# Down projection of an encoder layer: one token tile's share of product 7 moved between two tiles of product 4

## The chip, the cores and the metric

The kernel runs on one core of a Trainium2 chip. The core has five engines with queues of their own: TensorE (PE in the profile; its weight loads are shown as PEld), VectorE (DVE), ScalarE (ACT), GpSimd (POOL) and SyncE (SP), which issues most of the DMAs. Each engine takes its instructions in the order in which they were written, and engines wait for each other through semaphores. TensorE writes its results to PSUM, eight banks of 128 partitions by 512 float32 values here, and VectorE or ScalarE read them from there.

The metric is the device time of one execution in microseconds. The comparison is between the median of several runs of the kernel before and of the changed kernel. The profile is one execution, recorded by the hardware profiler.

## What is computed

The reference is one layer of a bidirectional encoder over 1024 tokens of width 1024: a mixing part (retention and windowed attention), a first layer norm that gives `h`, then a gated feed-forward part with a small embedding term, and a second layer norm.

```python
g = jnp.einsum('bsd,df->bsf', h, w_ffn_gate[i])
up = jnp.einsum('bsd,df->bsf', h, w_ffn_up[i])
ffn = jnp.einsum('bsf,fd->bsd', jax.nn.silu(g) * up, w_ffn_down[i])
...
h = _layer_norm(ALPHA * h + ffn + ple_gate * ple, ln2_gain[i], ln2_bias[i])
```

The change lies in the last two lines: the down projection (the product of the 1024 x 2816 hidden values with `w_ffn_down`, 2816 x 1024) and the second layer norm of the finished rows.

## The kernel before

**Matmuls in parts.** Each float32 operand is split into a high part and a rest (`split`, L74: ScalarE writes the high part on L75, VectorE the rest on L76), and a product takes three matmuls: high by high, high by rest, rest by high (`mm3c`, L891 to L893). Each has 128 x 128 stationary and 128 x 512 moving values.

**Seven products.** The down projection is computed with seven products in place of eight (a Strassen-like scheme on 2 x 2 blocks: two halves of the tokens, two halves of the hidden values, two halves of the output columns). A product `p` takes a combination of blocks of the hidden values (loaded from the scratch tensor `ad`) and a combination of blocks of `w_dn` (loaded, and summed by DMAs on GpSimd's queue that add in memory, L1222). `AIN` (L1188) says which part each product takes.

**Units.** The hidden dimension is cut in 11 pairs of 128-row blocks, in two segments: `SEG` (L1187) has pairs 0 to 4 and 5 to 10. A unit is one product for one pair; `seq` (L1401) gives the order, in which the second segment ends with products 3, 7 and 4. There are 77 units (`ND`). A unit has four steps: `dload` issues its loads, `dprep` splits its two operands into two slots of the ring `"op"`, `mm` does its matmuls for four token tiles of 128 rows, and `post` runs at the last pair of a product.

**Slots.** The ring `"op"` has 22 slots of one split operand each, taken in turn, so that a slot comes back after eleven units. `dprep` runs up to ten units ahead of `mm` (L1459 to L1461).

**Banks.** The four token tiles of a product accumulate in four PSUM banks. Products 6, 7 and 4 of the second segment share their four banks (`GRP`, L1360): product 7 adds to what product 6 left there, product 4 to both. At the end of products 6 and 7 `dpost` (L1362) adds or subtracts the banks as they then stand into the accumulators `accd` in SBUF (`addto`, L1274).

**The lower tiles and the upper tiles.** `accd` 0 to 3 are token tiles of the first half, 4 to 7 of the second. Tiles 4 to 7 are finished after product 3; their layer norm is laid out in `later` (L1390 to L1394), of which one list is popped in each of the following steps: `squares` and a multiply on ScalarE, `rstd` with a power on GpSimd (L1312), a product with the gain on VectorE (L1337), and an addition of the bias by DMA (L1338).

**The end.** The last product, 4, isn't done pair by pair over the four tiles: `products(t)` does its six pairs for one tile, and `tail` (L1342) goes through tiles 0 to 3, so that the layer norm of a tile runs beside the matmuls of the next. Its parts, on VectorE unless noted: `addto` with sums, `var` (mean, and for tiles 0 to 2 the squares on ScalarE, L1295), `rstd` (two small instructions, then the power on GpSimd), `center` (subtract the mean, times the gain, L1317, two halves), `scale` (times the reciprocal deviation, plus bias, L1322, two halves, each followed by its store on SP's queue, L1323). Tile 3 (`LAST`) takes its sums with `bn_stats` (L1282, L1301).

**Order.** From the gate and up projection on, PE, DVE, Activation, Pool and SP are under `manual_schedule` (L1468): each engine's queue has the order in which the program writes its instructions.

**Buffers `R`.** `dpost` of product 1 keeps four tiles of the tag `"w"` (L1369), from which twelve DMAs on GpSimd's queue add into the accumulators (L1376).

Of the kernel before, what the change touches and what calls it, by code (L numbers as in the profile page):

```python
# [10 lines left out]
F32R = mybir.dt.float32r  # L11
# [5 lines left out]
P = 128  # L17
# [4 lines left out]
HF = 512  # L22
# [20 lines left out]
def layer(tc, xT, xn, w_first, w_mt, w_rv, w_out, w_pg, w_pe, pT, w_gu, w_dn,  # L43
# [11 lines left out]
    wp = cstack.enter_context(tc.tile_pool(name="wp", bufs=4))  # L55
# [3 lines left out]
    def nm(s):  # L59
        uid[0] += 1  # L60
        return f"{s}{uid[0]}"

    def bank(tag, shape=(P, HF)):
        return ps.tile(list(shape), F32, tag=tag, bufs=NB[tag], name=nm("b" + tag))
# [36 lines left out]
    def rawt(w):  # L101
        return wp.tile([P, w], F32, tag="raw", bufs=2, name=nm("raw"))
# [51 lines left out]
    with tc.manual_schedule(engines={mybir.EngineType.DVE, mybir.EngineType.SP}):  # L154
        for kt in range(KT):
            r = xraw[kt]
# [25 lines left out]
            w = wf[kt % 2]  # L182
# [316 lines left out]
    class Attention:  # L499
# [62 lines left out]
        def half(self, hh):  # L562
            return self.y[:, hh * HF:(hh + 1) * HF].rearrange("p (n c) -> p n c", n=4)
# [76 lines left out]
    def ytile(k):  # L640
        ys[k] = a_tile([P, S], "y", "A0" if k < 4 else "A1")
        return ys[k]
# [39 lines left out]
    with tc.manual_schedule(engines={mybir.EngineType.PE}):  # L682
# [11 lines left out]
        r = Retention(0, y0)  # L694
# [6 lines left out]
        for i in range(1, NPAIR):  # L701
# [3 lines left out]
            r = Retention(i, ytile(2 * i))  # L705
# [19 lines left out]
    for n, k in enumerate(order):  # L725
        if n % 2 == 0:
            yp = big16()
        t = yp[:, :, n % 2, :]
# [64 lines left out]
    for kt in range(4):  # L793
        if kt % 2 == 0:
            wbig = ct([P, 2, 2, 2, HF], ("h2", "h3")[kt // 2], dt=F32R)
        r = rawt(2 * HF)
# [92 lines left out]
    def mm3c(o, lh, ll, rh, rl, start, stop):  # L889

        pe.matmul(o, lh, rh, start=start, stop=False, skip_group_check=True)  # L891
        pe.matmul(o, lh, rl, start=False, stop=False, skip_group_check=True)  # L892
        pe.matmul(o, ll, rh, start=False, stop=stop, skip_group_check=True)  # L893
# [269 lines left out]
    n = 0  # L1163
# [23 lines left out]
    SEG = [list(range(0, 5)), list(range(5, NP))]  # L1187
    AIN = {1: (3, 1), 2: (1, 1), 3: (1, 0), 4: (0, 1), 5: (2, 0), 6: (0, 0), 7: (3, 0)}  # L1188
    rings = {"op": [], "a": [], "chain": [], "b": []}
    turn = {k: 0 for k in rings}  # L1190
# [62 lines left out]
    def dmm(p, n, k, ts, first, stop):  # L1253

        a, b = dops[p, n]
        for t in ts:
            c = slice(t * P, (t + 1) * P)
            mm3c(dbank[k][t], a[:, 0, c], a[:, 1, c], b[:, 0, :], b[:, 1, :], first, stop)
# [8 lines left out]
    def pop():  # L1267
        for f in later.pop(0):
            f()
# [4 lines left out]
    def addto(t, h, b, op=ALU.add, done=False):  # L1274


        if done and t != LAST and op == ALU.add:
            dve.tensor_tensor_reduce(half(t, h), half(t, h), b, 1.0, 0.0, op, ALU.add, stts[t][:, h:h + 1])
            return
        dve.tensor_tensor(half(t, h), half(t, h), b, op)  # L1280
        if done and t == LAST:
            dve.bn_stats(stts[t][:, 6 * h:6 * h + 6], half(t, h))  # L1282
        elif done:
            act.activation(ct([P, HF], "sg", 2), half(t, h), AF.Copy, accum_out=stts[t][:, h:h + 1])

    LAST = 3

    def negmean(t):
        stt = stts[t]
        dve.tensor_scalar(stt[:, 12:13], stt[:, 0:1], stt[:, 1:2], -1.0 / D, ALU.add, ALU.mult)  # L1290

    def squares(t):
        stt = stts[t]
        for h in range(2):
            act.activation(ct([P, HF], "sg", 2), half(t, h), AF.Square, bias=stt[:, 12:13], accum_out=stt[:, 2 + h:3 + h])  # L1295

    def var(t):

        stt = stts[t]
        if t == LAST:  # L1300
            dve.bn_aggr(stt[:, 12:14], stt[:, 0:12])  # L1301
            dve.tensor_scalar(stt[:, 12:13], stt[:, 12:13], -1.0, None, ALU.mult)
        else:
            negmean(t)
            squares(t)

    def rstd(t):
        stt = stts[t]
        if t != LAST:
            dve.tensor_scalar(stt[:, 13:14], stt[:, 2:3], stt[:, 3:4], 1.0 / D, ALU.add, ALU.mult)  # L1310
        dve.tensor_scalar(stt[:, 14:15], stt[:, 13:14], EPS, None, ALU.add)
        pool.tensor_tensor(stt[:, 15:16], stt[:, 14:15], cst[:, C_MH:C_MH + 1], ALU.pow)  # L1312

    def center(t):
        for h in range(2):
            x = half(t, h)
            dve.scalar_tensor_tensor(x, x, stts[t][:, 12:13], ln2[0][:, hs[h]], ALU.add, ALU.mult)  # L1317

    def scale(t):
        for h in range(2):  # L1320
            x = half(t, h)
            dve.scalar_tensor_tensor(x, x, stts[t][:, 15:16], ln2[1][:, hs[h]], ALU.mult, ALU.add)  # L1322
            sp.dma_start(out[t][:, hs[h]], x)  # L1323
# [18 lines left out]
    def tail(products):  # L1342

        bs = dbank[len(SEG) - 1, GRP[4]]
        for t in range(4):
            products(t)
            if t:
                rstd(t - 1)
            addto(t, 0, bs[t], done=True)
            var(t)  # L1350
            if t < LAST:
                if t:
                    scale(t - 1)
                center(t)
        rstd(LAST)
        scale(LAST - 1)
        center(LAST)
        scale(LAST)

    GRP = {1: 0, 2: 0, 5: 1, 3: 1, 6: 2, 7: 2, 4: 2}  # L1360
# [1 line left out]
    def dpost(p, s, t):  # L1362

        last = s == len(SEG) - 1
        b = dbank[s, GRP[p]][t]
        if p == 1:
            if s == 0:
                if t % 2 == 0:
                    R.append([wp.tile([P, 2, HF], F32, tag="w", bufs=4, name=nm("R")) for _ in range(2)])  # L1369
                act.activation(R[t // 2][0][:, t % 2], b, AF.Copy)  # L1370
            else:
                r, n = (x[:, t % 2] for x in R[t // 2])
                dve.tensor_tensor(r, r, b, ALU.add)
                act.activation(n, r, AF.Copy, scale=-1.0)
                for tt, h, x in ((t, 0, r), (t + 4, 1, n), (t, 1, n)):
                    later.append([lambda o=half(tt, h), x=x: pool.dma_start(o, x, accum_op=ALU.add)])  # L1376
        elif p == 2:
            addto(t + 4, 0, b, done=last)
        elif p == 5:
            addto(t, 1, b)  # L1380
        elif p == 6:
            addto(t + 4, 1, b, ALU.subtract)
        elif p == 3:
            addto(t + 4, 1, b, done=last)
            if last:
                negmean(t + 4)
                if t == 0:
                    squares(4)
            if last and t == 3:
                f, m, w = ([x[i] for x in map(ln2_steps, range(4, NT))] for i in range(3))  # L1390
                q = [None] + [lambda u=u: squares(u) for u in range(5, NT)]
                later.extend([[], [q[1], f[0]], [m[0], w[0], q[2], f[1]], [m[1], w[1], q[3], f[2]], [m[2], f[3]], [m[3]],
                              [w[2], w[3]]])
                later[-1].extend(lambda u=u: sp.dma_start(out[u], accd[u]) for u in range(4, NT))  # L1394
        elif p == 7:
            addto(t, 1, b, ALU.subtract, done=last)
        else:
            addto(t, 0, b)


    seq = [(1, 0), (5, 0), (2, 0), (3, 0), (6, 0), (1, 1), (7, 0), (2, 1), (4, 0), (5, 1), (6, 1), (3, 1), (7, 1), (4, 1)]  # L1401
# [4 lines left out]
    def d_units(p, s):  # L1406
        k, first, grp, last = (s, GRP[p]), p in (1, 5, 6), SEG[s], (p, s) == seq[-1]

        def mm(n):
            if first and n == grp[0]:  # L1410
                tg = dsets[which[k]]
                dbank[k] = [bank(tg[t // 2]) for t in range(4)]
            if not last:
                dmm(p, n, k, range(4), first and n == grp[0], n == grp[-1])
            elif n == grp[-1]:
                def products(t):
                    for q in grp:
                        dmm(p, q, k, [t], False, q == n)

                while later:  # L1420
                    pop()
                tail(products)

        def post(n):
            if n == grp[-1] and not last:
                for t in range(4):
                    dpost(p, s, t)

        for n in grp:
            dunits.append((lambda n=n: dload(p, n), lambda n=n: dprep(p, n), lambda n=n: mm(n), lambda n=n: post(n)))  # L1430
# [4 lines left out]
    NG, ND = len(gunits), len(dunits)  # L1435
# [10 lines left out]
    def load_ln2():  # L1446
        for j in range(2):
            g = ct([P, D], "u", 4)
            sp.dma_start(g, lnp[2 + j].partition_broadcast(P))
            ln2.append(g)  # L1450

    def d_step(k):
        dunits[k][2]()
        dunits[k][3]()
        if later and k < ND - 6:
            pop()
        while stores and stores[0][0] <= NG + k:
            stores.pop(0)[1]()
        pa = min(10, 5 + k // 3)  # L1459
        ahead(0, k + 1 + pa + 4)  # L1460
        ahead(1, k + 1 + pa)  # L1461
        if k in (2, 3, 4, 5, 8, 9, 10, 11):
            load_acc()
        if k == ND - 24:
            load_ln2()

    ET = mybir.EngineType
    with tc.manual_schedule(engines={ET.PE, ET.DVE, ET.Activation, ET.Pool, ET.SP}):  # L1468
# [112 lines left out]
```

## Time and profile before

| what | value |
|---|---|
| runs | 1204.84 us median of 3 (1204.73 to 1205.9) |
| profiled execution | 1208.0 us, its span 1206.2 us |
| mean granted TensorE clock | 0.998 |
| DVE busy | 735.6 us (61%) |
| ACT busy | 507.6 us (42%) |
| POOL busy | 363.1 us (30%) |
| HBM read and written | 124.67 MB and 47.45 MB |

The span goes from the first to the last instruction of the profiled execution; the rest of its time lies around it. In a row of the timeline stand the start, the duration, the engine, the line, the operation, the tiles written and read, how many instructions are merged, and in brackets how long the engine was idle before and what released it. In a row of the stretches stand the length, the busy time and number of instructions of each engine, the granted clock, the busy share of the DMA engines and GB/s. The end of a matmul is modelled; the spacing of starts is what TensorE delivers.

### The profile page before, as it was taken

The numbers are of one execution on the slowest core, as the hardware profiler recorded it, in microseconds if no ns is written. First come the engines' busy times: TensorE is split into PE (matmuls) and PEld (weight loads), VectorE is DVE, ScalarE is ACT, GpSimd is POOL, SyncE is SP. The second block draws the span as 40 slices with busy tenths as digits, with TensorE's granted clock in tenths as the row PEclk, the third lists the DMA queues.
The fourth block names the chain that finished last, engine by engine and source line by source line (L and its number), as shares of the span: only waits on it lengthen the run. The fifth ranks groups of instructions, "written<-read, shape, count | busy, mean of one in ns | idle before, by whom it ended". The sixth has DMA issues, their size and how long they took to land.

```text
span 1206.2 us, 16452 instructions
## 1 busy us (share of the span) xinstructions
PE 1192.5 (99%) x5940; PEld 994.1 (82%) x5940; DVE 735.6 (61%) x1262; ACT 507.6 (42%) x958; POOL 363.1 (30%) x342
## 2 busy tenths in 40 slices
PE   9999999999999999999999999999999999999997
PEld 6888888888888888888888888888888888888885
DVE  4633788866645387946855554455554565775677
ACT  4665237665775124303423323233323324562463
POOL 2001020202010021001765565646656432034232
PEclk9999999999999999999999999999999999999999
DMA  6233635410103216656233222332133159999976
GB/s 249 83 110 141 249 135 195 151 40 20 35 18 122 91 50 229 255 202 220 89 132 131 79 79 105 131 132 79 63 121 131 70 178 300 375 274 218 258 178 199
DMA packets 70034, 178.45 MB, mean 148 GB/s; under 512 B 8128, under 2 KB 12352, under 8 KB 69952
## 3 DMA queue, kind: packets, MB, share of 16 engines
q1 hardware_dynamic: 61312, 160.61, 37.3%
q0 software_dynamic: 8640, 16.78, 8.0%
q8 instruction: 47, 0.77, 0.3%
q14 instruction: 35, 0.29, 0.1%
HBM read 124.67 MB, written 47.45 MB: 143 GB/s over the span
## 4 chain that ended last, share of the span: by engine, by line
PE 95%; DVE 2%; DMA 1%; issue 1%; ACT 1%; DVEq 0%; SPq 0%; ACTq 0%
PE bmm L81 7%; PE bmm L83 7%; PE bmm L82 7%; PE bs L893 5%; PE bs L891 5%; PE bs L892 5%; PE bmm L891 5%; PE bmm L892 5%; PE bmm L893 5%; PE bt L891 5%; PE bt L893 5%; PE bt L892 5%; PE bo L891 4%; PE bo L893 4%; PE bo L892 4%; PE bo L557 2%
## 5 line engine op out<-in xcount | busy, mean ns | idle before, releaser
L81 PE MATMUL bmm<-H,w 128*128 128x512 f32 x240 | 97.0, 404 | 1.4 <-ACT H L75 1.4
L83 PE MATMUL bmm<-H,w 128*128 128x512 f32 x240 | 94.4, 393 | 0.0
L82 PE MATMUL bmm<-H,w 128*128 128x512 f32 x240 | 94.0, 392 | 0.0
L1050 POOL TENSOR_TENSOR H<-ln 128x512 f32<-128x512 f32 x22 | 28.9, 1313 | 180.9 <-ACT w L75 98.0
L76 DVE TENSOR_TENSOR w<-raw,w 128x512 fp32r<-128x512 f32 x64 | 51.0, 804 | 51.3 <-ACT w L75 50.8
L1080 POOL TENSOR_TENSOR ev<-ev 128x512 f32<-128x512 f32 x33 | 55.0, 1666 | 90.5 <-DVE ev L1095 39.4
L76 DVE TENSOR_TENSOR w<-H,w 128x512 fp32r<-128x512 f32 x44 | 41.0, 932 | 62.5 <-ACT w L75 62.5
L518 POOL COPY sc<-skb 128x1 f32<-128x1 f32 x64 | 14.3, 229 | 193.0 <-PE bt L545 143.9
L1078 ACT ACTIVATE ev<-ev 128x512 f32<-128x512 f32 x33 | 20.9, 632 | 102.7 <-DVE ev L1095 102.7
L1084 POOL TENSOR_TENSOR ev<-ev,ev 128x512 f32<-128x512 f32 x44 | 62.7, 1437 | 2.6
L76 DVE TENSOR_TENSOR u<-H,u 128x512 fp32r<-128x512 f32 x47 | 36.7, 781 | 37.7 <-ACT u L75 37.4
L81 PEld LDWEIGHTS bmm<-H,w 128*128 128x128 f32 x240 | 45.2, 188 | 11.6 <-ACT H L75 2.4
L83 PEld LDWEIGHTS bmm<-H,w 128*128 128x128 f32 x240 | 45.2, 188 | 10.0
L523 DVE CUSTOM_DVE_ANT_0 sc<-cst,bs,skb 128x384 f32<-128x384 f32 (+1 forms) x64 | 34.8, 577 | 28.8 <-PE bs L522 27.0
L75 ACT ACTIVATE w<-raw 128x512 fp32r<-128x512 f32 x64 | 39.3, 624 | 30.2 <-PE bo L83 12.4
L82 PEld LDWEIGHTS bmm<-H,w 128*128 128x128 f32 x240 | 45.3, 189 | 7.8
L527 ACT ACTIVATE sc<-sc,st 128x385 f32<-128x385 f32 (+1 forms) x64 | 37.2, 584 | 32.2 <-DVE st L525 32.2
L75 ACT ACTIVATE u<-H 128x512 fp32r<-128x512 f32 x47 | 29.6, 630 | 44.6 <-PE bs L893 8.1
L763 POOL TENSOR_TENSOR stt<-stt,cst 128x1 f32<-128x1 f32 x8 | 11.6, 1456 | 101.0 <-DVE stt L762 101.0
L479 POOL TENSOR_TENSOR sm<-sm,cst 128x8 f32<-128x8 f32 x8 | 14.3, 1783 | 88.3 <-DVE sm L478 88.3
L1054 POOL TENSOR_TENSOR H<-raw,H 128x512 f32<-128x512 f32 x22 | 37.3, 1697 | 0.0
L1051 POOL TENSOR_TENSOR H<-H,raw 128x512 f32<-128x512 f32 x22 | 35.7, 1624 | 1.7
(807 smaller groups left out, 3748.1 us busy)
## 6 DMA issues: line engine op xcount, KB each, us to landing
ad<-ev SPq DMA_DIRECT2D x33, 512.0 KB, 2.6
pgd<-pro SPq DMA_DIRECT2D x28, 512.0 KB, 2.9
raw<-in_w_gu SPq DMA_DIRECT2D x22, 512.0 KB, 4.3
ln<-in_w_gu SPq DMA_DIRECT2D x22, 512.0 KB, 3.6
raw<-ad SPq DMA_DIRECT2D x40, 256.0 KB, 5.8
ln<-ad SPq DMA_DIRECT2D x37, 256.0 KB, 6.2
H<-in_w_dn SPq DMA_DIRECT2D x33, 256.0 KB, 6.1
raw<-in_w_mt SPq DMA_DIRECT2D x14, 512.0 KB, 3.8
```

The lines of the kernel that those rows point to most:

```text
L75: act.activation(hi, raw, AF.Copy)
L76: dve.tensor_tensor(lo, raw, hi.bitcast(F32), ALU.subtract)
L81: pe.matmul(o, lh, rh, start=start, stop=False)
L82: pe.matmul(o, lh, rl, start=False, stop=False)
L83: recent[0] = pe.matmul(o, ll, rh, start=False, stop=stop).ins.name
L527: act.activation(sc[g][:, :nk + 1], sc[g][:, :nk + 1], AF.Exp, bias=st_[:, 1, j, g:g + 1], accum_out=st_[:, 2, j, g:g + 1])
L891: pe.matmul(o, lh, rh, start=start, stop=False, skip_group_check=True)
L892: pe.matmul(o, lh, rl, start=False, stop=False, skip_group_check=True)
L893: pe.matmul(o, ll, rh, start=False, stop=stop, skip_group_check=True)
L1054: pool.tensor_tensor(s[3], a(0, 1), s[0], ALU.subtract)
L1080: pool.tensor_tensor(c[:, 1, :], c[:, 0, :], c[:, 1, :], ALU.mult)
L1084: pool.tensor_tensor(self.ev[dst][:, 0, :], left, right, op)
```

## The change

Product 7 of the second segment, the last but one, does its six pairs for tiles 0 to 2 alone, and `dpost` reads those three banks. Its part for tile 3 is now a call of `products(7, t)` in `tail`, between tiles 2 and 3 of product 4, followed by `scale(2)` and by the `dpost` of that tile. `rstd(2)` is written ahead of the moved matmuls; `scale(2)` is written between them and the matmuls of product 4 for tile 3; `rstd(3)` now comes behind `center(3)`. At step `ND - 32` four tiles of the tag `"w"` are put into the ring `"op"`, at the place that is next in turn, so that the ring has 26 slots.

```diff
         bs = dbank[len(SEG) - 1, GRP[4]]
         for t in range(4):
-            products(t)
-            if t:
+            if t == LAST:
+                rstd(t - 1)
+                products(7, t)
+                scale(t - 1)
+                dpost(7, len(SEG) - 1, t)
+            products(4, t)
+            if 0 < t < LAST:
                 rstd(t - 1)
             addto(t, 0, bs[t], done=True)
             var(t)
-            if t < LAST:
-                if t:
-                    scale(t - 1)
-                center(t)
+            if 0 < t < LAST:
+                scale(t - 1)
+            center(t)
         rstd(LAST)
-        scale(LAST - 1)
-        center(LAST)
         scale(LAST)
...
+        tiles = range(3 if (p, s) == seq[-2] else 4)
+
         def mm(n):
...
             if not last:
-                dmm(p, n, k, range(4), first and n == grp[0], n == grp[-1])
+                dmm(p, n, k, tiles, first and n == grp[0], n == grp[-1])
             elif n == grp[-1]:
-                def products(t):
+                def products(p, t):
                     for q in grp:
                         dmm(p, q, k, [t], False, q == n)
...
             if n == grp[-1] and not last:
-                for t in range(4):
+                for t in tiles:
                     dpost(p, s, t)
...
+        if k == ND - 32:
+            r, pos = rings["op"], turn["op"] % len(rings["op"])
+            r[pos:pos] = [wp.tile([P, 2, HF], F32R, tag="w", bufs=4, name=nm("w")) for _ in range(4)]
+            turn["op"] = pos
```

## The prediction

> **What bounds the kernel now.** I read the page's busy shares first, then the table of stretches over the last 42 us, then the end of the chain of work that ended last.
>
> ```profile
> PE 1192.5 (99%) x5940; PEld 994.1 (82%) x5940; DVE 735.6 (61%) x1262; ACT 507.6 (42%) x958; POOL 363.1 (30%) x342
> ...
> 1164.50:1180.80 16.30, 16.30 (x73) 13.51 (x72) 11.89 (x31) 12.10 (x25) 5.64 (x10) 1.00 0.48 103
> 1180.80:1197.30 16.50, 16.50 (x73) 13.33 (x71) 14.18 (x30) 8.06 (x20) 2.93 (x6) 1.00 0.84 236
> 1197.30:1206.20 8.90, 0.00 (x1) 0.00 (x0) 5.78 (x11) 0.00 (x0) 1.48 (x2) 0.73 0.36 133
> ```
>
> The columns of the last three rows are PE, PEld, DVE, ACT and POOL. TensorE is full until 1197.3: product 7 fills 1164.50 to 1180.82, product 4 the rest. Then 8.9 us follow without it, in which VectorE finishes token tile 3 and the last store lands. So the time is matmul time, plus any hole in it, plus that tail. The end of the chain:
>
> ```profile
> 1197.34 0.70 DVE acc L1280
> 1198.06 0.71 DVE stt L1282
> ...
> 1199.25 1.32 DVE acc L1322 x2
> 1200.57 0.72 DVE acc L1317 x2
> ...
> 1201.81 0.74 DVE acc L1322
> ```
>
> The 1.32 us of L1322 at 1199.25 are `scale(2)`, work of another tile inside tile 3's tail. The change takes it out of there, and pays with TensorE's order.
>
> **The matmuls.** They are neither added nor removed. The TensorE timeline gives their spacing:
>
> ```profile
> 1164.50 0.39 PE L891 MATMUL bs<-u,u 128*128 128x512 f32 x1
> ...
> 1180.82 0.39 PE L891 MATMUL bs<-H 128*128 128x512 f32 x1
> ...
> 1193.06 0.39 PE L891 MATMUL bt<-H 128*128 128x512 f32 x1
> ...
> 1196.92 0.39 PE L893 MATMUL bt<-u,u 128*128 128x512 f32 x1
> ```
>
> 72 matmuls take 16.32 us, 0.2267 each; one token tile of one product (six operands, three matmuls each) takes 18 of them, 4.08 us. Product 7 on three tiles thus ends its issue at 1164.50 + 54 x 0.2267 = 1176.74, 4.08 earlier than now, and 4.08 us of product 7 come back after product 4's third tile. Without a hole TensorE would end where it does now.
>
> **First hole, before product 4.** Products 6, 7 and 4 accumulate in the same four banks, and `dpost` has to read a bank between 7 and 4. What VectorE does there now:
>
> ```profile
> 1176.64 1.23 DVE L1337 TENSOR_TENSOR acc<-acc,u 128x1024 f32<-128x1024 f32 x1 [1.98 <-ACT acc L1334]
> 1177.78 0.21 DVE L1310 TENSOR_SCALAR stt<-stt 128x1 f32<-128x1 f32 x1
> ...
> 1178.33 0.15 DVE L1311 TENSOR_SCALAR stt<-stt 128x1 f32<-128x1 f32 x1
> 1178.98 1.37 DVE L1280 TENSOR_TENSOR acc<-acc,bs 128x512 f32<-128x512 f32 x2 [0.50 <-PE bs L893]
> ```
>
> At 1178.98 it reads tile 0's bank, after 0.50 us of waiting for TensorE. That 0.50 is all the slack. Ahead of the read in the same queue stand the upper tiles' normalizing steps, and these go by their own chain, not by TensorE:
>
> ```profile
> 1175.13 0.20 POOL L1331 TENSOR_TENSOR stt<-stt 128x1 f32<-128x1 f32 x1
> 1175.36 1.25 ACT L1334 ACTIVATE acc<-acc,stt 128x1024 f32<-128x1024 f32 x1 [1.51 <-POOL stt L1331]
> ```
>
> GpSimd's L1331 ends at 1175.33 and releases ScalarE's L1334 0.03 later, which releases VectorE's L1337 at 1176.64. Further back this chain hangs on a DMA: the last split ahead of product 3's evictions waited for its operand.
>
> ```profile
> 1162.59 0.63 ACT L75 ACTIVATE H<-h0b 128x512 fp32r<-128x512 f32 x1 [0.59 <-DMA h0b<-in_w_dn]
> ```
>
> So taking product 7's fourth tile away moves TensorE up and not VectorE. The read can begin 0.07 after the start of the L1311 at 1178.33 (0.06 is what an independent instruction follows it by in the rows of the tail, below), at 1178.40, and ends 0.69 later (half of the 1.37 for two), at 1179.09. What a matmul pays when VectorE releases it shows in one place:
>
> ```profile
> 578.19 1.77 DVE L76 TENSOR_TENSOR w<-H,w 128x512 fp32r<-128x512 f32 x1
> ...
> 580.02 0.50 PE L893 MATMUL bs<-H,w 128*128 128x512 f32 x1 [0.35 <-DVE w L76]
> 580.36 0.39 PE L891 MATMUL bs<-H,w 128*128 128x512 f32 x1
> ```
>
> It starts 0.06 after VectorE's end (579.96), and the next one follows after 0.34 instead of 0.23: 0.11 more. Product 4 therefore starts at 1179.15 instead of 1176.74, and the hole is 2.41 + 0.11 = **2.52 us**. The evictions of tiles 1 and 2 end at 1180.5, long before their banks are written. Tile 0 of product 4 then ends about 1183.5; VectorE is free for it when the last L1337 is through:
>
> ```profile
> 1180.08 2.38 ACT L1334 ACTIVATE acc<-acc,stt 128x1024 f32<-128x1024 f32 x2 [2.06 <-POOL stt L1331]
> ...
> 1189.18 0.69 DVE L1278 CUSTOM_DVE_ANT_0 acc<-acc,bs 128x512 f32<-128x512 f32 x1 [0.34 <-PE bs L893]
> ```
>
> 1182.46 + 1.23 = 1183.7. These 0.2 us are taken up by the 0.34 for which VectorE waits ahead of the next tile, and cost nothing.
>
> **Second hole, before tile 3 of product 4.** The moved 18 matmuls end 4.08 us after product 4's tile 2. Their bank must again be read by VectorE before product 4 may add to it, and here nothing else is left for TensorE. What is queued in front of that read, by the rows of tile 2 now:
>
> ```profile
> 1193.26 0.69 DVE L1278 CUSTOM_DVE_ANT_0 acc<-acc,bt 128x512 f32<-128x512 f32 x1 [0.17 <-PE bt L893]
> ...
> 1194.12 1.40 DVE L1322 SCALAR_TENSOR_TENSOR acc<-acc,stt,u 128x512 f32<-128x512 f32 x2
> ...
> 1195.45 1.41 DVE L1317 SCALAR_TENSOR_TENSOR acc<-acc,stt,u 128x512 f32<-128x512 f32 x2
> ...
> 1196.77 0.21 DVE L1310 TENSOR_SCALAR stt<-stt 128x1 f32<-128x1 f32 x1
> 1197.01 0.15 DVE L1311 TENSOR_SCALAR stt<-stt 128x1 f32<-128x1 f32 x1
> 1197.25 0.55 POOL L1312 TENSOR_TENSOR stt<-stt,cst 128x1 f32<-128x1 f32 x1 [3.53 <-DVE stt L1311]
> ```
>
> `addto(2)` starts 0.20 after the slot in which TensorE's next matmul goes out (1193.06). From there to the end of GpSimd's L1312 is 4.54 (1197.80), all of it one chain: sums, mean, `scale(1)`, `center(2)`, `rstd(2)`. Then come, in the new order, `scale(2)`, which is 0.03 behind GpSimd (as L1334 behind L1331) and lets the next instruction start after 1.33 (1194.12 to 1195.45), and only then the read of tile 3's bank, 0.69. Sum from the free slot: 0.20 + 4.54 + 0.03 + 1.33 + 0.69 = 6.79, and 0.06 to release TensorE: 6.85. The moved matmuls cover 4.08 of it. The hole is 2.77, with the slow second matmul 0.11 more: **2.88 us**. Of the 6.79, what has no row is the empty VectorE behind L1312; its length is that of GpSimd's power, for which there are eight cases:
>
> ```profile
> L1312 POOL TENSOR_TENSOR stt<-stt,cst x8: 545/560/1341, 1169.0 to 1199.3; 128x1 f32<-128x1 f32 x8
> ```
>
> I take the 0.55 of tile 2's row above; with 1.34 the hole is 0.8 larger. From below: had VectorE nothing in front of the read, the hole would be 0.20 + 0.69 + 0.06 + 0.11 = 1.06. The bn_stats that follows the read lies beside the last 18 matmuls, as do the two stores of `scale(2)` on SP's queue.
>
> **The tail.** After its mean (L1302) tile 3 now goes on with `scale(2)`, and the power runs beside that:
>
> ```profile
> 1199.04 0.15 DVE L1302 TENSOR_SCALAR stt<-stt 128x1 f32<-128x1 f32 x1
> 1199.11 0.14 DVE L1311 TENSOR_SCALAR stt<-stt 128x1 f32<-128x1 f32 x1
> 1199.17 1.40 DVE L1322 SCALAR_TENSOR_TENSOR acc<-acc,stt,u 128x512 f32<-128x512 f32 x2
> ```
>
> Afterwards `center(3)` follows L1302, and `rstd(3)` has been moved behind it, so that the power is no longer covered by anything. From `addto(3)` to the first half of `scale(3)` it is now 1201.81 - 1197.34 = 4.47. Then: L1302 ends at 1.85, `center(3)` starts at 1.88, L1311 follows it by 1.32 at 3.20 and ends at 3.35, GpSimd starts 0.09 later (1197.16 to 1197.25) and ends at 3.99, `scale(3)` starts at 4.02. **Gain 0.45 us** of the 1.32 that left; the rest goes to the uncovered power. With the slowest power (1.34) it is a loss of 0.34. From `scale(3)` on nothing changes.
>
> **The four slots.** They are the buffers of `R`, whose last additions are DMAs on GpSimd's queue. Twelve operands of product 7 stay alive to the end now, so without the slots the last split would overwrite one. The buffer that comes free last goes to the split that stands here at 1129.44 and waits for its own DMA:
>
> ```profile
> 1117.20 0.87 POOL L1376 DMA_DIRECT2D acc<-R  x1 [2.72 <-issue]
> ...
> 1129.44 0.64 ACT L75 ACTIVATE H<-h 128x512 fp32r<-128x512 f32 x1 [2.17 <-DMA h<-in_w_dn]
> ...
> DMA to landing us min/median/max: 4.4/5.6/8.9
> ```
>
> The last of the twelve additions is issued at 1117.20; the slowest landing gives 1126.1, the median 1122.8. I cost the wait at nothing; its cover is 3.3 to 6.6 us. If that is gone, what queues behind is every later split on ScalarE and VectorE, and through them the chain of the first hole.
>
> **Sum.** 2.52 + 2.88 - 0.45 = +4.95 us on the profiled span of 1206.2, so 1211.1. That execution took 1208.0 with what lies around the span, 3.2 over the runs' median of 1204.84; I put the difference on the median: 1204.84 + 4.95 = **1209.8 us**, 0.4% slower.
>
> **Rivals.**
>
> *Only the second hole.* The first one depends on when the upper tiles' chain lets VectorE go, and that hangs on DMA landings (1162.59). If the chain runs 2.5 us earlier in the changed kernel, which has more slots and so splits sooner, 2.88 - 0.45 = +2.4 remain: 1207.3. Against it: ScalarE's waits there are for DMAs, not for slots.
>
> *Not slower.* One mechanism: VectorE is early enough that the read of a bank follows its last matmul at once. Its place is the read of tile 3; from 1.8 us less in front of it on, nothing but the 1.06 is left, and with the first hole gone too the sum is 1.06 - 0.45 = +0.6: 1205.4. For it speaks only that VectorE is 14.18 of 16.50 us busy in that stretch, not full; against it that the 4.54 are a chain of dependences. That the change does what it says without any wait of TensorE would give -0.45, 1204.4; the shared bank excludes it.
>
> *The clock falls in the holes.* The profile shows the granted clock fall when TensorE has been idle:
>
> ```profile
> 1199.30:1201.30 2.00, 0.00 (x0) 0.00 (x0) 2.00 (x4) 0.00 (x0) 0.99 (x1) 1.00 0.27 101
> 1201.30:1203.30 2.00, 0.00 (x0) 0.00 (x0) 1.92 (x3) 0.00 (x0) 0.00 (x0) 0.51 0.45 165
> ```
>
> It is 1.00 up to 4.0 us after the last matmul and 0.51 from then on. The holes last 2.5 and 2.9 us, so I expect no fall; if it came in the second one all the same, the 18 matmuls behind it would take up to 4.08 more: 1213.9. [...]
>
> *The slots wait.* Late landings of `R` push the splits, and the first hole grows by as much: with 2 us, 1211.8.
>
> **How the numbers follow.** Chances: forecast 0.66 (own range 1208.4 to 1211.2, from a power of 0.55 to 1.34 and a chain 1 us earlier or later), only the second hole 0.13, not slower 0.05, clock 0.07, slots 0.09. The range is 1206.9 to 1212.0: it holds the forecast, the second hole alone and most of the slots. About 0.2% (2.4 us) is what a measurement of this kernel can tell from no change. The second hole alone lies on that edge, so half of its chance counts as no change: same 0.06 + 0.04 = 0.10, slower 0.88; faster 0.02, the small rest of the not-slower case, since no term here is worth 2.4 us downward.
>
> **What the changed profile would show.** TensorE with two idle times, each released by VectorE's L1280 or its like: some 2.4 us ahead of product 4's first matmul, some 2.8 us ahead of its last 18. VectorE without idle time before product 7's first eviction (0.50 now). An idle VectorE of about 0.6 us before `scale(2)` and again before `scale(3)`. The last matmul about 5.4 us later than now, and the tail behind it about 0.45 shorter. The prediction is wrong if TensorE goes from product 7 to product 4 without a hole, if VectorE reads tile 3's bank ahead of `scale(2)`, or if the clock falls.

## The result, and the profile after

| | before | changed |
|---|---|---|
| median of 6 runs | 1204.78 us | 1214.75 us |
| lowest and highest | 1204.29, 1206.2 | 1211.78, 1217.96 |
| profiled execution, its span | 1208.0, 1206.2 | 1216.79, 1215.0 |
| its mean granted clock | 0.998 | 0.994 |

The ratio is 1.008, with an interval of 1.0068 to 1.0091. The forecast was slower by 4.95 us; it became some 10, outside the range of 1206.9 to 1212.0.

TensorE's waits in the changed kernel, in the view that groups them (total, times, longest), show the two holes first:

```profile
PE bs L891 <- DVE acc L1280: 3.2, 1, 3.2
PE bt L891 <- DVE acc L1280: 2.6, 1, 2.6
```

Both end with a read of a bank by VectorE (L1280). The timeline of TensorE at these places:

```profile
1174.96 0.39 PE L893 MATMUL bt<-w,w 128*128 128x512 f32 x1
1178.57 0.77 PE L891 MATMUL bs<-h0a 128*128 128x512 f32 x1 [3.22 <-DVE acc L1280]
1179.13 0.63 PE L892 MATMUL bs<-h0a 128*128 128x512 f32 x1
1179.56 0.63 PE L893 MATMUL bs<-h0a 128*128 128x512 f32 x1
...
1185.56 0.40 PE L891 MATMUL bs<-h0a 128*128 128x512 f32 x1
...
1197.58 0.39 PE L893 MATMUL bt<-w,w 128*128 128x512 f32 x1
1200.56 0.50 PE L891 MATMUL bt<-h0a 128*128 128x512 f32 x1 [2.59 <-DVE acc L1280]
...
1202.01 0.63 PE L893 MATMUL bt<-H 128*128 128x512 f32 x1
1202.43 0.63 PE L891 MATMUL bt<-H 128*128 128x512 f32 x1
...
1206.18 0.40 PE L893 MATMUL bt<-H 128*128 128x512 f32 x1
```

The matmul before a hole holds its slot for 0.23 us, so TensorE is free at 1175.19 and at 1197.81, and the holes are 3.38 and 2.75 us long. Behind the first of them at once, and behind the second from the fifth matmul on, matmuls follow each other by about 0.43 instead of 0.23: tile 0 of product 4 takes 6.99 us (1178.57 to 1185.56) instead of 4.08, tile 3 takes 5.85. On VectorE and GpSimd in the same execution:

```profile
1177.67 0.15 DVE L1311 TENSOR_SCALAR stt<-stt 128x1 f32<-128x1 f32 x1
1177.74 1.27 DVE L1280 TENSOR_TENSOR acc<-acc,bs 128x512 f32<-128x512 f32 x2
...
1197.91 0.55 POOL L1312 TENSOR_TENSOR stt<-stt,cst 128x1 f32<-128x1 f32 x1 [3.53 <-DVE stt L1311]
1198.50 1.41 DVE L1322 SCALAR_TENSOR_TENSOR acc<-acc,stt,u 128x512 f32<-128x512 f32 x2 [0.66 <-POOL stt L1312]
1199.83 0.68 DVE L1280 TENSOR_TENSOR acc<-acc,bt 128x512 f32<-128x512 f32 x1
...
1206.61 0.69 DVE L1280 TENSOR_TENSOR acc<-acc,bt 128x512 f32<-128x512 f32 x1 [5.38 <-PE bt L893]
...
1210.64 1.41 DVE L1322 SCALAR_TENSOR_TENSOR acc<-acc,stt,u 128x512 f32<-128x512 f32 x2 [0.66 <-POOL stt L1312]
```

The first read stands right behind the upper tiles' L1311, with no idle time. The second waits for GpSimd's power and for `scale(2)`. The tail from `addto(3)` to `scale(3)` is 4.03 us. The slow matmuls (0.43 us apart) go with a lower granted clock (0.50). In these stretches the third number from the end is the granted clock:

```profile
1177.50:1178.00 0.50, 0.00 (x0) 0.00 (x0) 0.47 (x4) 0.00 (x0) 0.38 (x1) 0.74 0.29 115
1184.50:1184.75 0.25, 0.25 (x2) 0.20 (x2) 0.00 (x0) 0.00 (x0) 0.00 (x0) 0.86 1.09 344
1201.50:1201.75 0.25, 0.25 (x3) 0.20 (x2) 0.00 (x0) 0.00 (x0) 0.00 (x0) 0.77 0.33 107
1205.00:1205.25 0.25, 0.25 (x2) 0.22 (x1) 0.00 (x0) 0.00 (x0) 0.00 (x0) 0.90 0.00 0
1211.50:1212.00 0.50, 0.00 (x0) 0.00 (x0) 0.50 (x1) 0.00 (x0) 0.00 (x0) 0.88 0.00 0
```

The clock goes from 1.00 to 0.50 inside the first of these rows, back in the second, down again in the third, back in the fourth, and down in the tail in the last (the values between the steps stand in the windows further below). A row's mean places the step: 0.74 over 0.50 us is 0.24 at full and 0.26 at half, so the step is at 1177.74. In the same way the others are at 1184.57, 1201.63, 1205.05 and 1211.88. The first fall comes inside its hole, the second 1.1 us after its hole has ended.

From profile to profile the time divides like this (us; slots are counted as above):

| term | forecast | profiles |
|---|---|---|
| TensorE comes to the end of product 7 | 0 | -1.55 (1175.19 for 1176.74) |
| first hole | +2.41 | +3.38 |
| tile 0 of product 4 slower | +0.11 | +2.91 |
| second hole | +2.77 | +2.75 |
| tile 3 of product 4 slower | +0.11 | +1.77 |
| behind the last matmul | -0.45 | -0.46 |
| sum | +4.95 | +8.80 |

### The profile page after: what moved, and what is told of

Same layout as the page of the kernel before. It is cut to its first block, busy times and chain, and to the rows that moved or that the text cites. A ratio compares the mean times of both kernels' runs of the same rounds, so it can differ in the third digit from the quotient of the medians.

```text
span 1215.0 us, 16451 instructions
## 1 busy us (share of the span) xinstructions
PE 1196.9 (99%) x5940; PEld 996.5 (82%) x5940; DVE 734.6 (60%) x1262; ACT 507.6 (42%) x958; POOL 361.0 (30%) x342
## 4 chain that ended last, share of the span: by engine, by line
PE 89%; issue 3%; DVE 3%; DMA 3%; POOL 1%; ACT 1%; POOLq 0%; DVEq 0%; SPq 0%; ACTq 0%
PE bmm L81 7%; PE bmm L82 7%; PE bmm L83 7%; PE bs L891 5%; PE bs L893 5%; PE bs L892 5%; PE bmm L892 5%; PE bmm L893 5%; PE bmm L891 5%; PE bt L892 4%; PE bt L891 4%; PE bt L893 4%; PE bo L892 4%; PE bo L891 4%; PE bo L893 4%
## 5 line engine op out<-in xcount | busy, mean ns | idle before, releaser
L81 PE MATMUL bmm<-H,w 128*128 128x512 f32 x240 | 97.0, 404 | 0.0
L81 PEld LDWEIGHTS bmm<-H,w 128*128 128x128 f32 x240 | 45.2, 188 | 10.0 <-ACT H L75 0.8
L75 ACT ACTIVATE w<-H 128x512 fp32r<-128x512 f32 x46 | 28.6, 622 | 22.2 <-PE bs L893 6.3
```

What stands on the lines that cost most here:

```text
L75: act.activation(hi, raw, AF.Copy)
L81: pe.matmul(o, lh, rh, start=start, stop=False)
```

## The experiments

Each ran against the kernel before on the same chip, whose median was 1205.07, 1205.17 and 1205.61 us in the three groups.

### The read ahead of `scale(2)`

```diff
                 products(7, t)
-                scale(t - 1)
                 dpost(7, len(SEG) - 1, t)
+                scale(t - 1)
```

> The changed kernel with one swap: VectorE reads tile 3's bank (dpost of product 7) ahead of scale(2) instead of behind it. Theory (the granted clock is set in a grid of 3.41 us windows and halves when TensorE was idle for most of one): the second hole shrinks from 2.86 us to about 1.06 (0.20 + 0.69 + 0.06 + 0.11), no window is then mostly idle there, and tile 3's 18 matmuls take 4.08 instead of 5.85; the first hole stays at 2.4 to 3.4 with its slow tile 0. Together 1.8 + 1.8 = 3.6 us less than the changed kernel: about 1211.2. Rival (the slow matmuls come from something other than idle time, such as DMA traffic beside them): only the hole shrinks, 1.8 us less, about 1213, and tile 3's matmuls stay slow.

Measured: 1211.32 us (1208.88 to 1213.49), ratio 1.005 (1.0035 to 1.0064), 3.4 less than the changed kernel. TensorE at both holes:

```profile
1173.03 0.39 PE L893 MATMUL bt<-w,w 128*128 128x512 f32 x1
1178.30 0.77 PE L891 MATMUL bs<-h0a 128*128 128x512 f32 x1 [4.88 <-DVE acc L1280]
...
1196.63 0.39 PE L893 MATMUL bt<-w,w 128*128 128x512 f32 x1
1197.79 0.50 PE L891 MATMUL bt<-h0a 128*128 128x512 f32 x1 [0.78 <-DVE acc L1280]
1198.13 0.39 PE L892 MATMUL bt<-h0a 128*128 128x512 f32 x1
```

The second hole is 0.93 us, and the matmuls behind it run at their usual spacing (0.23 us from the second on). The first hole is 5.04 us here, where 2.4 to 3.4 was expected: TensorE came to it 1.9 us earlier than in the changed kernel's profile, and VectorE only 0.3. So the first hole isn't of a fixed length, and that the time came out as expected is in part luck.

### Matmuls without use in both holes

```diff
+    def fill(count):
+        db = bank("mm")
+        a, b = dops[7, SEG[-1][0]]
+        for _ in range(count):
+            pe.matmul(db, a[:, 0, 0:P], b[:, 0, :], start=True, stop=True)
...
                 dpost(7, len(SEG) - 1, t)
+                fill(10)
             products(4, t)
...
                 dmm(p, n, k, tiles, first and n == grp[0], n == grp[-1])
+                if (p, s) == seq[-2] and n == grp[-1]:
+                    fill(12)
```

> The changed kernel with matmuls into an unused PSUM bank in both holes: 12 after product 7's three tiles (2.72 us) and 10 after its part for tile 3 (2.27 us). Their results are not used. VectorE's waits stay as they are. Theory (idle time halves the clock): the useful matmuls start at the same times as in the changed kernel, but at the full clock: tile 0 and tile 3 of product 4 take 4.08 us each, 2.9 + 1.8 = 4.7 us less, about 1210, near the forecast of 1209.8, the runs lie closer together than 1211.8 to 1218.0, and the mean granted clock of all runs is 0.997 or more. Rival (DMA traffic beside the matmuls slows them): no gain, 1214 to 1215, and tile 0's matmuls still 0.43 us apart.

Measured: 1210.78 us (1209.44 to 1212.48), ratio 1.0046 (1.0033 to 1.006), the clock of its four runs 0.997 or 0.998. Its timeline of TensorE:

```profile
1173.68 2.88 PE L1346 MATMUL bmm<-h 128*128 128x512 f32 x12
1176.94 0.47 PE L891 MATMUL bs<-h0a 128*128 128x512 f32 x1 [0.38 <-DVE acc L1280]
1177.25 0.39 PE L892 MATMUL bs<-h0a 128*128 128x512 f32 x1
...
1193.38 2.43 PE L1346 MATMUL bmm<-h 128*128 128x512 f32 x10
1196.13 0.50 PE L891 MATMUL bt<-h0a 128*128 128x512 f32 x1 [0.32 <-DVE acc L1280]
1196.47 0.40 PE L892 MATMUL bt<-h0a 128*128 128x512 f32 x1
```

The useful matmuls still stand still, for 3.26 us (1173.68 to 1176.94) and 2.75 us, and then run 0.23 to 0.24 us apart from the second on. More work on TensorE made the kernel 4.0 us faster. That is what the clock cost, since the holes stayed about as long (3.26 and 2.75 us for 3.38 and 2.75). The rival, DMA traffic that slows the matmuls, is excluded: behind both holes they keep the spacing of the full clock (0.23 us at 1.00 in the changed kernel). What is left, 5.7 us over before, is near the forecast's 4.95.

### The four slots alone

```diff
+        if k == ND - 32:
+            r, pos = rings["op"], turn["op"] % len(rings["op"])
+            r[pos:pos] = [wp.tile([P, 2, HF], F32R, tag="w", bufs=4, name=nm("w")) for _ in range(4)]
+            turn["op"] = pos
```

> The kernel before with the four more operand slots and nothing else. Theory (the slots cost nothing: the last addition from R lands 3.3 us or more before the split that takes its buffer): 1204.8, within 0.2% of before. Rival (the slots delay the splits, and so the chain that VectorE's read hangs on): slower than before by up to 2 us, since only 0.5 us of slack stands ahead of the read there.

Measured: 1205.48 us (1203.77 to 1207.46), ratio 1.0003 (0.9994 to 1.0012). In the kernel before, the slots cost nothing that can be measured; the interval leaves room for 1.4 us.

### The upper tiles' products behind the evictions

```diff
-                later.extend([[], [q[1], f[0]], [m[0], w[0], q[2], f[1]], [m[1], w[1], q[3], f[2]], [m[2], f[3]], [m[3]],
-                              [w[2], w[3]]])
+                later.extend([[], [q[1], f[0], q[2], f[1]], [m[0], q[3], f[2], w[0]], [m[1], f[3]], [m[2]], [m[3]],
+                              [w[1], w[2], w[3]]])
```

> The changed kernel with the upper tiles' steps laid out otherwise: the statistics of tiles 5 and 6 one step earlier, and the products with the gain of tiles 5 to 7 (L1337 there) behind product 7's evictions instead of ahead of them, so that VectorE comes to the first eviction some 2 us earlier. Theory (the first hole is VectorE's in-order queue, held up by the upper tiles' chain): the first hole falls from 2.4 to 3.4 us to at most 1.4, tile 0's matmuls run at the full clock, the second hole stays at 2.9 to 3.6 with or without its slow matmuls: 4 to 5.5 us less than the changed kernel, 1209 to 1211. Rival (the read waits for something else, such as DMA landings): the first hole stays above 2.4 us.

Measured: 1209.56 us (1207.63 to 1212.94), ratio 1.0038 (1.0024 to 1.0053). In its profile TensorE goes from product 7 to product 4 without a hole:

```profile
1173.81 0.39 PE L893 MATMUL bt<-w,w 128*128 128x512 f32 x1
1174.04 0.40 PE L891 MATMUL bs<-h0a 128*128 128x512 f32 x1
```

So the first hole was VectorE's queue. The second was there as before, from 1190.38 to 1193.13, and this time the clock did not fall after it. In this profile the clock falls at 1202.00, in the tail; three times 3.41 us before that is 1191.76, inside the hole. Taken from there, the windows on both sides have TensorE busy for 64 and 60%, and the clock (third number from the end) stays at 1.00:

```profile
1188.35:1191.76 3.41, 2.19 (x10) 1.49 (x8) 2.71 (x7) 0.71 (x3) 0.55 (x1) 1.00 0.60 235
1191.76:1195.17 3.41, 2.04 (x9) 1.71 (x10) 2.01 (x4) 0.00 (x0) 0.00 (x0) 1.00 1.01 380
```

Why such windows matter is worked out further below. The five runs fall apart by their clock: 1207.63 and 1207.70 us at 0.998, the other three, 1209.56 to 1212.94, at 0.997 or 0.996. The two are where the second hole alone was forecast (+2.4 us).

### Both orders together

The edits of the first and the fourth experiment in one kernel.

> The changed kernel with both orders of e4 and e1: the upper tiles' products behind product 7's evictions, and the read of tile 3's bank ahead of scale(2). Theory: no first hole, a second hole of 0.95 to 1.06 us, the clock full in every run, and the tail 0.45 shorter: 0.5 to 0.6 us over before, about 1205.6, no change that can be measured, with a spread like that of before (about 3 us). Rival (something else of the change costs time too): over 1207.

Measured: 1206.94 us (1205.38 to 1210.46), ratio 1.0019 (1.001 to 1.0028): that is 1.8 us over before, 1.2 more than expected. The interval, 1206.4 to 1208.5 us, holds the rival's 1207, so the rival isn't excluded. In its profile (of a run of 1206.1 us) a first hole of 0.33 us is left; other runs are up to 4.4 us longer, and their traces weren't taken.

### A bank of its own for tile 3

As the kernel with both orders together, and:

```diff
                 dpost(7, len(SEG) - 1, t)
+                addto(t, 0, bs[t])
                 scale(t - 1)
+                bs[t] = bank("o")
...
+            if t == LAST:
+                rstd(t)
             center(t)
-        rstd(LAST)
         scale(LAST)
...
-                        dmm(p, q, k, [t], False, q == n)
+                        dmm(p, q, k, [t], p == 4 and t == LAST and q == grp[0], q == n)
```

> As f1, but product 4's part for tile 3 goes into a bank of its own, so that it waits for no read; the shared bank is added in one more VectorE instruction beside those matmuls, and rstd(3) is put ahead of center(3) again, so that the power is covered. Theory: no hole at all, and of the tail the whole of scale(2) goes, 1.2 to 1.3 us: about 1203.8, faster than before by 0.1%. Rival (VectorE can't keep up with what now lies beside the last 18 matmuls): addto(3) is late, and the gain is eaten: 1205 or more.

Measured: 1205.14 us (1203.8 to 1207.26), ratio 1.0 (0.9991 to 1.0008). The second hole is gone, and the tail is as worked out: in this profile VectorE's `addto(3)` and `scale(3)` are 3.22 us apart, 1.25 less than in the kernel before.

```profile
1195.57 0.69 DVE L1280 TENSOR_TENSOR acc<-acc,bo 128x512 f32<-128x512 f32 x1 [0.75 <-PE bo L893]
...
1198.79 1.41 DVE L1322 SCALAR_TENSOR_TENSOR acc<-acc,stt,u 128x512 f32<-128x512 f32 x2
```

But the first hole is back, with 1.69 us (its last matmul of product 7 started at 1172.93):

```profile
1174.85 0.47 PE L891 MATMUL bs<-h0a 128*128 128x512 f32 x1 [1.53 <-DVE acc L1280]
```

The time is one that the rival named, but not for its reason: `addto(3)` waited 0.75 us for TensorE, so VectorE kept up. In this profile the gain went into the first hole. Against the profile of the fourth experiment, which has no such hole, TensorE came 0.88 us earlier and VectorE 0.89 later (its read at 1174.03 for 1173.14).

### One hole, filled

The fourth experiment with `fill(10)` in the second hole.

> As e4, with 10 matmuls into an unused bank in the second hole; their results are not used. Theory (what spreads e4's runs from 1207.6 to 1212.9 is whether the clock falls in its one hole): 2.86 - 0.45 = 2.4 us over before in every run, about 1207.5, spread no wider than that of before. Rival (e4's spread has another cause): spread as in e4, median about 1209.5.

Measured: 1208.53 us (1207.47 to 1212.81), ratio 1.0043 (1.003 to 1.0057). Four of seven runs lie between 1207.47 and 1208.53, near the theory. Three are at 1212 to 1213, so the spread did not go, and the theory doesn't account for it: two of the three have a clock of 0.996, the third has 0.998 like the fast ones. The profile still has a first hole, of 1.28 us, which was not filled. That the three runs had a longer one would fit, but none was profiled, and their cause stays open.

### TensorE made late

```diff
                 dbank[k] = [bank(tg[t // 2]) for t in range(4)]
+                if (p, s) == (6, 1):
+                    a, b = dops[p, n]
+                    for _ in range(13):
+                        pe.matmul(dbank[k][0], a[:, 0, 0:P], b[:, 0, :], start=True, stop=True)
```

> The changed kernel with 13 more matmuls (2.95 us) at the start of product 6 of the second segment, overwritten by the first matmul of that product, so that TensorE comes 2.95 us later to product 4. Theory (the first hole ends when VectorE is ready, at a time that TensorE doesn't set): the hole is 2.95 us shorter, or gone, and with it mostly its slow tile 0: no slower than the changed kernel, rather 1 to 4 us faster, 1211 to 1214. Rival (the hole is a wait of fixed length behind TensorE's own matmuls): 2.95 us slower than the changed kernel, about 1217.7.

Measured: 1213.87 us (1212.92 to 1215.62), ratio 1.0074 (1.0061 to 1.0087). TensorE at the first hole:

```profile
1176.87 0.39 PE L893 MATMUL bt<-w,w 128*128 128x512 f32 x1
1178.37 0.47 PE L891 MATMUL bs<-h0a 128*128 128x512 f32 x1 [1.11 <-DVE acc L1280]
1178.67 0.39 PE L892 MATMUL bs<-h0a 128*128 128x512 f32 x1
```

2.95 us of extra matmuls did not make the kernel slower, so the rival is excluded. The hole shrank to 1.27, and the matmuls behind it keep their spacing of 0.23 us. The hole ends when VectorE is ready, at 1178.3 here, 1178.5 in the changed kernel, 1178.2 in the first experiment (1176.9 in the second, whose VectorE was early). But the theory's "at a time that TensorE doesn't set" is not the whole of it. In this profile VectorE waited for the end of product 3 before it began the upper tiles' evictions:

```profile
1163.01 0.69 DVE L1278 CUSTOM_DVE_ANT_0 acc<-acc,bo 128x512 f32<-128x512 f32 x1 [1.38 <-PE bo L893]
```

So a late TensorE makes VectorE's chain late too, and by this profile some 1.3 us of the first hole would stay, however late TensorE came (an estimate: no run was later).

### Four of six pairs

As the kernel with the bank of its own, with two of product 7's pairs for tile 3 left in their place.

```diff
-                dmm(p, n, k, tiles, first and n == grp[0], n == grp[-1])
+                dmm(p, n, k, range(4) if n in grp[:2] else tiles, first and n == grp[0], n == grp[-1])
...
-                    for q in grp:
+                    for q in grp[2 * (p == 7):]:
```

> As f2, but only four of product 7's six pairs for tile 3 are moved (2.72 us of matmuls), two stay in their place (1.36 us). Theory (what eats f2's gain is the rest of the first hole, 1.7 us in its profile, because TensorE still comes there before VectorE): that hole falls to 0.3 us; VectorE had 0.75 us to spare ahead of addto(3) in f2 and is now some 0.6 late. Net 0.7 to 0.8 us less than f2, about 1204.4, at the edge of what these runs can tell from before. Rival (f2's gain is lost elsewhere): as f2, 1205.1.

Measured: 1204.99 us (1203.49 to 1207.16), ratio 0.9997 (0.9988 to 1.0006). It can't be told from before, nor from the kernel without the edit: the interval, 1204.2 to 1206.3 us, holds the theory's 1204.4 and the rival's 1205.1. The forecast of the hole missed. It is still 1.34 us in this profile, where 0.3 was expected, as VectorE came to its read 2 us later than in the profile of the kernel without the edit. Its queue shows why. The chain of the upper tiles starts with ScalarE's last split ahead of product 3's evictions. In the profile of the kernel with the bank of its own:

```profile
1160.73 0.63 ACT L75 ACTIVATE H<-h0b 128x512 fp32r<-128x512 f32 x1
...
1174.03 1.27 DVE L1280 TENSOR_TENSOR acc<-acc,bs 128x512 f32<-128x512 f32 x2
```

With four of six pairs:

```profile
1162.68 0.64 ACT L75 ACTIVATE H<-h0b 128x512 fp32r<-128x512 f32 x1 [0.17 <-DMA h0b<-in_w_dn]
...
1176.00 1.27 DVE L1280 TENSOR_TENSOR acc<-acc,bs 128x512 f32<-128x512 f32 x2
```

The read starts 13.3 us after that split in both, and 13.3 or 13.4 after it in the three other profiles with this order. In the order of the changed kernel it is 15.8: the read at 1177.74 belongs to this split.

```profile
1161.95 0.63 ACT L75 ACTIVATE H<-h0b 128x512 fp32r<-128x512 f32 x1 [0.72 <-DMA h0b<-in_w_dn]
```

It is 15.8 as well in the first two experiments and, up to the 1178.40 at which the read could have begun, in the kernel before; where TensorE was made late it is 17.3, with the wait of 1.38 us. So the first hole is the difference of two times that vary from one execution to the next: when this split comes, between 1159.5 and 1162.7 in the eleven profiles, and when TensorE comes to the end of product 7.

## Why the prediction was wrong

**What held.** That the change makes the kernel slower, and why. Both holes are where they were put, each ended by the read that was named, behind the instructions that were named. The second hole was forecast at 2.77 us and measured at 2.75, the tail at 4.02 and 4.03. The slots cost nothing that could be measured.

**The step that failed: "The holes last 2.5 and 2.9 us, so I expect no fall".** The case had the fall of the clock as a rival at 0.07, and in the second hole alone. In the profiles it fell in the first and 1.1 us behind the second, and took 2.80 + 1.66 us of the 8.8 (the 2.91 and 1.77 above, without the 0.11 each of restarting). By medians, the kernel with filled holes says 4.0 of 10. The step read the tail of the kernel before, where the clock was 1.00 up to 4.0 us after the last matmul, as a limit on the length of a hole. It is not one. The five steps of the clock in the changed kernel are 6.83, 17.06, 3.42 and 6.83 us apart, which is 2, 5, 1 and 2 times 3.41: they lie on a grid, and what the clock did at its points went with the window just past. The windows of the changed kernel, in which the first number behind the length is TensorE's busy time:

```profile
1174.33:1177.74 3.41, 1.02 (x5) 0.52 (x3) 1.69 (x5) 2.65 (x5) 0.39 (x3) 1.00 0.62 118
1177.74:1181.15 3.41, 2.58 (x6) 2.13 (x7) 2.34 (x5) 1.74 (x2) 2.25 (x5) 0.50 1.00 269
1181.15:1184.57 3.42, 3.42 (x9) 2.65 (x9) 1.90 (x2) 2.48 (x7) 1.75 (x2) 0.50 0.56 176
...
1198.22:1201.63 3.41, 1.07 (x5) 0.88 (x6) 2.70 (x4) 0.00 (x0) 0.24 (x1) 1.00 0.41 153
1201.63:1205.05 3.42, 3.42 (x10) 2.68 (x9) 0.00 (x0) 0.00 (x0) 0.00 (x0) 0.50 0.01 3
1205.05:1208.46 3.41, 1.53 (x7) 0.92 (x5) 1.74 (x4) 0.00 (x0) 0.00 (x0) 1.00 0.00 0
```

With 1.02 and 1.07 us busy of 3.41 (30 and 31%) the clock fell at the end of the window; with 1.53 (45%) it did not. It came back after a window that was busy throughout, not after one with 2.58 (76%). Two of the other profiles read the same way. These rows hold the fall and the return in the first experiment, then those with the late TensorE:

```profile
1176.00:1176.50 0.50, 0.00 (x0) 0.00 (x0) 0.50 (x1) 0.50 (x3) 0.00 (x0) 0.51 0.22 33
1182.50:1183.00 0.50, 0.50 (x2) 0.37 (x2) 0.27 (x1) 0.50 (x3) 0.43 (x1) 0.66 0.00 0
...
1197.50:1198.00 0.50, 0.44 (x2) 0.34 (x3) 0.47 (x2) 0.00 (x0) 0.00 (x0) 0.79 0.90 316
1201.00:1201.50 0.50, 0.50 (x3) 0.46 (x2) 0.00 (x0) 0.00 (x0) 0.00 (x0) 0.80 0.00 0
```

Placed as above, the falls are at 1176.01 and 1197.79 and the returns at 1182.84 and 1201.20, which is 2 and 1 times 3.41 later, and in the 3.41 us before each fall TensorE was busy for 0.82 (24%). In the profile of the bank of its own, where the matmuls behind the hole keep their 0.23 us, any 3.41 us that hold the 1.53 us for which TensorE was idle have 1.88 busy (55%). So the hole of 2.75 us cost no more than its length in the fourth experiment, where it lay across a point of the grid (1191.76), and 1.66 us more in the changed kernel, where most of it lay inside one window. In the tail of the kernel before, the 4.0 us were the rest of one window and a whole one:

```profile
1194.52:1197.94 3.42, 2.78 (x13) 1.97 (x11) 3.21 (x7) 1.30 (x4) 0.55 (x1) 1.00 0.90 338
1197.94:1201.35 3.41, 0.00 (x0) 0.00 (x0) 3.31 (x9) 0.00 (x0) 0.99 (x1) 1.00 0.18 66
...
1201.00:1201.50 0.50, 0.00 (x0) 0.00 (x0) 0.50 (x2) 0.00 (x0) 0.00 (x0) 0.85 0.97 348
```

The last row puts that fall at 1201.35, behind a window without any matmul; the window ahead of it, with 2.78 us busy (81%), was followed by none.

**The other step that was short: the base.** "I put the difference on the median" took the 3.2 us between the profiled execution and the median as the same in both kernels. The group of L81 in the input projection (its first and last start stand behind the durations) says where they arose. In the kernel before, in the changed one, and in the kernel before with the four slots alone, whose profiled execution took 1204.61 us, close to the median of before:

```profile
L81 PE MATMUL bmm<-H,w x240: 387/389/794, 6.4 to 374.7; 128*128 128x512 f32 x120
```

```profile
L81 PE MATMUL bmm<-H,w x240: 387/389/796, 4.8 to 372.3; 128*128 128x512 f32 x120
```

```profile
L81 PE MATMUL bmm<-H,w x240: 387/389/796, 4.6 to 371.5; 128*128 128x512 f32 x120
```

In the profile of before TensorE began 1.6 us later than in the changed kernel's, and it reached the last of these matmuls 2.4 us later. Against the kernel with the slots it was 3.2 us late there, and its span is 3.5 us longer (1206.2 for 1202.7): TensorE sets the end in both, and a late start counts nearly in full. (It had waited 1.45 us for a split of ScalarE, and its matmuls were 0.43 us apart until 9.93, in the kernel with the slots only until 5.20. The granted clock reads 1.00 there in both, so the cause of that spacing isn't shown.) In the changed kernel VectorE sets the end of the first hole, and a TensorE that starts early only waits longer (3.38 and 5.04 us in two profiles; 1.27 where it was made late). In the table TensorE is 1.55 us early and VectorE's release 0.58 (1178.51 for the 1179.09 of the forecast), which makes the first hole 0.97 longer. The 5.7 us that remain without the clock are 0.75 over the forecast, of the right sign and size for this; how much of them it is wasn't separated.

**The rivals.** The case of the second hole alone came true only where the chain was laid out otherwise. The not-slower case has no part in it: both reads were late. The slots' case has their run against it, in the kernel before; in the changed kernel's profile no split of ScalarE between 1100 and 1150 us waits for an addition from `R`.

## What to carry to other kernels

Moving matmuls away from in front of a read of their bank took away the time that VectorE needed here, and left holes of 3.38 and 2.75 us; look up what stands ahead of the read in its queue, and try a bank of its own for work that must follow such a read (here the second hole was gone with it). A hole on TensorE cost its length here and, by where it lay, matmuls 0.43 for 0.23 us apart behind it during one or two windows of 3.41 us; filling it with matmuls into an unused bank, 4.0 us faster in the median, told the two apart in one run. And a profiled execution that is slower than the median is not simply a constant to be added: ask which engine was late in it, and whether that engine still sets the end after the change.

## What the runs showed of the hardware

In the changed kernel's profile the five steps of the granted clock, between 1.00 and 0.50, lie on a grid of 3.41 us. Its place differed from one execution to the next: the falls at 1201.35 (the kernel before), 1176.01 (the first experiment), 1202.00 (the fourth) and 1197.79 (the late TensorE) lie 6.92, 0.51, 7.11 and 5.87 times 3.41 us from the step at 1177.74 there. Windows with 24 to 31% of matmul time let it fall, and so did those with none in the tails; those with 45% and more that the rows above show at the full clock did not. Holes of 0.93 to 1.7 us were never followed by a fall in the profiles above, one of 2.75 us was in two profiles (the changed kernel and the late TensorE) and was not in a third (the fourth experiment). Coming back took one window (3.41 us) where the window was full, and two (6.83 us) where TensorE began 0.83 us into the first (the changed kernel) or 2.29 us into it (the first experiment). With the clock go the changed kernel's runs, which spread by 6.2 us (1211.78 to 1217.96), the shortest of them with a mean clock of 0.997 and the others with 0.994 to 0.996, while the six of the kernel before spread by 1.9 (by 3.4 in the largest group of its runs, 26).
